# Feed forward of a hybrid diffusion step: tensor operations moved from GpSimd to VectorE and ScalarE, second weights prepared in the first product, loads issued ahead of splits

## Chip, cores and metric

The kernel runs on one core of one Trainium2 chip. The metric is the time of the device in microseconds (us). PE is TensorE, DVE is VectorE, ACT is ScalarE, POOL is GpSimd, SP is SyncE, whose only work here is to issue loads.

## What is computed

One layer over 128 context tokens and 2048 latent tokens, in fp32. A norm, a projection, three groups of mixing (gated linear attention, a depthwise convolution, chunked gating) and an output projection come first; the change is nearly all in what follows:

```python
h = rmsnorm(x, norm2_g) * (1 + scale2) + shift2
x = x + gate2 * (jnp.square(jax.nn.relu(h @ w_ff1)) @ w_ff2)   # 1024 -> 4096 -> 1024
y = rmsnorm(x, final_g)
```

## The kernel before

**Arithmetic.** Each fp32 operand is split into two halves in the fast matmul format: ACT copies it rounded (`hi`, an ACT CAST in the profile), and a subtraction gives the rest (`lo`). A product takes three matmuls (`mm3`: hi by hi, hi by lo, lo by hi). Both products of the feed forward use a seven-product scheme for 2x2 blocks in place of eight products, so that sums and differences of blocks are operands too.

**First product** (`ff1_units`, tiles `T`/`u` and `v`). Two groups of tokens, g = 0 and 1, times 16 column blocks i of `w_ff1`. One such turn has seven products p0 to p6 of 4 units of 3 matmuls, 84 matmuls of 512 columns; in group 0 a turn has 24 more of 256 columns for the context tokens (`ff1_context`). All seven read right operands made of tokens, which stay for a whole group (`right_operand`, tiles T for p0 to p3, u for p4 to p6), and left operands made of weights, which are new for each turn (`left_operand`: two loads into `raw`, the sums, four splits into `v`). The results lie in four banks z: p0, p2, p4 and p6 write one and the same bank, p3 and p5 another one, p1 a bank g. After each product ACT or DVE takes the bank away (`after(p)`: copies by ACT after p0, p2 and p3, additions by DVE after p1, p4 and p5). p4 can't begin before the copy after p2 is done, nor p6 before the addition after p4. Squares of the positive part, then three combinations of blocks (`comb`, on GpSimd) follow, and stores of the tiles fx, fy, fz to `f_d`.

**Second weights** (`w2_prep`). `w_ff2` times gate2 and its block combinations are made on GpSimd, 16 times (2 operations of 128x1024, 4 of 128x512, 7 stores to `w_d`), 3 times in group 1 of the first product and 13 times in the second product.

**Second product** (`ff2_units`, tiles `o`, `s`). Eight parts c of the hidden columns times four groups b of tokens, 84 matmuls each, and 24 more per c for the context tokens (`context`). Every operand is loaded from `f_d` or `w_d` and split (`operand`, lines 1405 and 1406; the subtraction goes to DVE or GpSimd by a rule). After each product DVE adds the bank to the sum of its tokens (line 1510, two for each p). Two of the z banks are held by the context tokens.

**Order.** `weave(units, items)` runs items between the units of the matmuls at hand-written positions; a scheduler then orders each engine's instructions, which the engine runs in that order. SP issues loads in the order of the program, and a load waits in SP's queue for its buffer. Stores go through POOL's queue. The relations that matter most are these two, from `weave` and `after`:

```python
while items and items[0][0] <= i:
    items.pop(0)[1]()          # a position of an item is a number of units
u()
bank = (za, gb, za, zc, za, zc, za)   # which bank p0 to p6 write
```

Of the kernel before, what the change touches and what calls it, by code (L numbers as in the profile page):

```python
# [43 lines left out]
def tile_hybrid(  # L44
# [62 lines left out]
    def raw():  # L107
        return rawp.tile([P, D], F32, tag="raw", name="raw", bufs=3)
# [4 lines left out]
    def cacc():  # L113
        return rawp.tile([P, D], F32, tag="cacc", name="cacc", bufs=2)
# [646 lines left out]
    def stage(t):  # L761
# [415 lines left out]
    def split_in_place(hi, lo, eng=V):  # L1177
        S.copy(out=hi, in_=lo.bitcast(F32))
        eng.tensor_tensor(out=lo, in0=lo.bitcast(F32), in1=hi.bitcast(F32), op=ALU.subtract)

    def right_operand(g, i, kk, dst):

        unit = tunit if i < 4 else uunit
        hi, lo = unit(), unit()
        ld_in_order(out=lo.bitcast(F32).rearrange("p (k n) -> p k n", k=2), in_=tb_d[g][:, i, 2 * kk:2 * kk + 2])
        split_in_place(hi, lo, G if kk else V)
        dst[i, kk] = (hi, lo)

    for t in range(NT - 2, -1, -1):
# [4 lines left out]
        if t in (3, 1, 0):  # L1194

            items += [((10 if t else 5) + 4 * kk, lambda kk=kk, i={3: 0, 1: 1, 0: 2}[t]: right_operand(0, i, kk, TB[0]))
                      for kk in range(2)]
# [21 lines left out]
    def left_operand(i):  # L1219

        w, rw, sf = {}, {}, {}
# [6 lines left out]
        def plain(r):  # L1228
            hi, lo = wunit(), wunit()
            split(hi, lo, rw[r])  # L1230
            w[r] = [x.rearrange("p (k f n) -> p k f n", k=4, f=2) for x in (hi, lo)]

        def sums(r):
            a1, a2 = (rw[x].rearrange("p (k f n) -> p k f n", k=4, f=2) for x in range(2))
            sf[r] = cacc()
            s_ = sf[r].rearrange("p (k f n) -> p k f n", k=4, f=2)
            if r == 0:

                V.tensor_tensor(out=s_[:, :, 0], in0=a1[:, :, 1], in1=a2[:, :, 1], op=ALU.add)
                V.tensor_tensor(out=s_[:, :, 1], in0=s_[:, :, 0], in1=a1[:, :, 0], op=ALU.subtract)  # L1240
            else:

                s2_ = sf[0].rearrange("p (k f n) -> p k f n", k=4, f=2)[:, :, 1]
                V.tensor_tensor(out=s_[:, :, 0], in0=a1[:, :, 0], in1=a1[:, :, 1], op=ALU.subtract)
                V.tensor_tensor(out=s_[:, :, 1], in0=a2[:, :, 0], in1=s2_, op=ALU.subtract)

        def mixed(r):
            hi, lo = wunit(), wunit()
            split(hi, lo, sf[r])
            w[2 + r] = [x.rearrange("p (k f n) -> p k f n", k=4, f=2) for x in (hi, lo)]  # L1250

        return w, [lambda: load(0), lambda: load(1), lambda: plain(0), lambda: plain(1),
                   lambda: sums(0), lambda: mixed(0), lambda: sums(1), lambda: mixed(1)]


    LEFT = ((0, 0), (1, 0), (2, 1), (2, 0), (3, 0), (3, 1), (1, 1))

    def ff1_units(g, i, w, tb):
# [12 lines left out]
        def square(x):  # L1271
            stt(x, x, 0.0, x, ALU.max, ALU.mult)

        def comb(out, a, b, op):
            G.tensor_tensor(out=out, in0=a, in1=b, op=op)  # L1275

        def after(p):
            if p == 0:
                S.copy(out=f00, in_=za)
            elif p == 1:  # L1280
                V.tensor_tensor(out=f00, in0=f00, in1=gb, op=ALU.add)
# [5 lines left out]
            elif p == 4:  # L1287
                V.tensor_tensor(out=f11, in0=fy[:, 0], in1=za, op=ALU.add)  # L1288
                square(f11)
            elif p == 5:  # L1290
                V.tensor_tensor(out=f01, in0=f01, in1=zc, op=ALU.add)
                square(f01)
                V.tensor_tensor(out=fy[:, 0], in0=f01, in1=f11, op=ALU.add)
# [359 lines left out]
```

## Time and profile before

| what | value |
|---|---|
| median of 3 runs | 2496.91 us (2488.81 to 2501.26) |
| profiled execution, its own time | 2490.42 us |
| its span, first to last instruction | 2488.7 us |
| mean granted TensorE clock | 0.967 |
| busy PE, DVE, POOL, ACT | 91%, 72%, 42%, 39% of the span |
| moved by DMA | 437.99 MB, mean 176 GB/s |

The feed forward takes the span from some 976 us on: group 0 of the first product until some 1361 us, group 1 until 1727 us, then the second product. An engine's share is an average over these stages, and a matmul's busy time includes its pipeline, so what a stage could gain is read from PE's waits and from the pace of its matmuls.

### The profile page before, as it was taken

Reading aid. Unit: us, or ns where it says so; the run is one execution under the profiler, and the core shown is the slowest. Engines: PE = TensorE matmul, PEld = TensorE weight load, DVE = VectorE, ACT = ScalarE, POOL = GpSimd, SP = SyncE. Lnnn points to the kernel's source line nnn. Section 1 sums busy time; section 2 is a strip of 40 time slices with the busy share of each in tenths; the row PEclk is TensorE's granted clock in tenths of the full one; section 3 lists DMA queues with packets and bytes.
Section 4 is the critical chain, followed back from the end, with each engine's and each line's share of the span. In section 5 each row is a group of like instructions: output and inputs, shape, how many; then the busy total and the mean of one; then the engine's idle time right before and its main releaser. Section 6 shows DMA issues by size and latency. Waiting matters only on the chain. (4 is left out here: it accounts for less than half of the span.)

```text
span 2488.7 us, 32998 instructions
## 1 busy us (share of the span) xinstructions
PE 2271.3 (91%) x12018; PEld 1854.0 (74%) x12018; DVE 1801.8 (72%) x2702; ACT 974.9 (39%) x1787; POOL 1055.8 (42%) x982
## 2 busy tenths in 40 slices
PE   6999999999988998899999789888889989989996
PEld 5788887777766776688887568677678777778775
DVE  5987755878887865677776787775667766677677
ACT  4666764333344465333333323222233233233242
POOL 2332325444424454333334454433655545545632
PEclk9999999999989999899999999999999999999999
DMA  8656635333445467333446345447666456456554
GB/s 283 235 196 200 218 103 172 121 126 125 139 148 196 144 221 250 123 128 122 140 138 219 133 153 169 157 148 263 213 208 218 165 186 198 166 192 203 173 203 144
DMA packets 217731, 437.99 MB, mean 176 GB/s; under 512 B 17525, under 2 KB 118175, under 8 KB 213984
## 3 DMA queue, kind: packets, MB, share of 16 engines
q1 hardware_dynamic: 171456, 263.57, 31.9%
q0 software_dynamic: 46112, 172.31, 19.8%
q8 instruction: 95, 1.56, 0.3%
q14 instruction: 68, 0.56, 0.1%
HBM read 270.39 MB, written 165.43 MB: 175 GB/s over the span
## 5 line engine op out<-in xcount | busy, mean ns | idle before, releaser
L131 PE MATMUL z<-w,hb 128*128 128x512 f32 (+1 forms) x2486 | 556.8, 370 | 14.7 <-ACT hb L776 8.8
L131 PEld LDWEIGHTS z<-w,hb 128*128 128x128 f32 x2486 | 418.6, 191 | 90.3 <-ACT hb L776 9.0
L131 PE MATMUL z<-u,v 128*128 128x512 f32 x1152 | 288.6, 407 | 57.3 <-DVE fz L1288 28.2
L131 PEld LDWEIGHTS z<-u,v 128*128 128x128 f32 x1152 | 224.5, 197 | 114.6 <-DVE fz L1288 31.8
L1405 ACT CAST o<-o 128x1024 fp32r<-128x1024 f32 x148 | 155.4, 1051 | 366.4 <-DMA o<-f_d 248.4
L131 PE MATMUL z<-T,v 128*128 128x512 f32 x1152 | 280.4, 395 | 10.4 <-ACT v L176 5.5
L1275 POOL TENSOR_TENSOR fz<-fx,fy 128x512 f32<-128x512 f32 x64 | 117.6, 1837 | 364.5 <-DVE fy L67 336.8
L131 PE MATMUL g<-o 128*128 128x512 f32 x1116 | 270.6, 391 | 0.5 <-DVE o L1406 0.5
L1510 DVE TENSOR_TENSOR T<-T,z 128x512 f32<-128x512 f32 x256 | 171.6, 682 | 137.0 <-PE z L131 136.9
L131 PE MATMUL z<-o 128*128 128x512 f32 x1080 | 265.1, 394 | 2.6 <-DVE T L1510 1.5
L131 PEld LDWEIGHTS z<-T,v 128*128 128x128 f32 x1152 | 216.7, 190 | 56.0 <-ACT v L176 5.7
L131 PEld LDWEIGHTS g<-o 128*128 128x128 f32 x1116 | 211.1, 189 | 45.4 <-DVE o L1406 1.0
L131 PEld LDWEIGHTS z<-o 128*128 128x128 f32 x1080 | 205.7, 191 | 48.5 <-DVE T L1510 3.2
L67 DVE SCALAR_TENSOR_TENSOR cacc<-xp,wd,cacc 128x512 f32<-128x512 f32 (+2 forms) x360 | 241.3, 724 | 0.1
L131 PE MATMUL z<-o,s 128*128 128x512 f32 x576 | 157.2, 417 | 55.7 <-DVE T L1510 27.4
L131 PE MATMUL z<-w,T 128*128 128x512 f32 x720 | 182.1, 406 | 6.0 <-ACT T L776 3.7
L1406 DVE TENSOR_TENSOR o<-o 128x1024 fp32r<-128x1024 f32 x96 | 165.8, 1729 | 20.8 <-ACT o L1405 20.5
L131 PEld LDWEIGHTS z<-o,s 128*128 128x128 f32 x576 | 113.2, 200 | 89.3 <-DVE T L1510 29.9
L1510 DVE TENSOR_TENSOR T<-T,g 128x512 f32<-128x512 f32 x192 | 130.0, 683 | 63.0 <-PE g L131 62.3
L131 PEld LDWEIGHTS z<-w,T 128*128 128x128 f32 x720 | 136.1, 194 | 34.6 <-ACT T L776 3.9
L1406 POOL TENSOR_TENSOR o<-o 128x1024 fp32r<-128x1024 f32 x52 | 128.2, 2475 | 60.9 <-ACT o L1405 60.5
L177 DVE TENSOR_TENSOR v<-cacc,v 128x1024 fp32r<-128x1024 f32 x64 | 78.2, 1222 | 103.4 <-ACT v L176 103.4
(312 smaller groups left out, 3608.6 us busy)
## 6 DMA issues: line engine op xcount, KB each, us to landing
o<-f_d SPq DMA_DIRECT2D x93, 512.0 KB
raw<-in_w_ff_dram SPq DMA_DIRECT2D x68, 512.0 KB
w_d<-T POOLq DMA_DIRECT2D x112, 256.0 KB, 3.1
o<-w_d SPq DMA_DIRECT2D x55, 512.0 KB
f_d<-fz POOLq DMA_DIRECT2D x32, 768.0 KB, 5.9
raw<-in_w_mod_dram SPq DMA_DIRECT2D x32, 512.0 KB
f_d<-fy POOLq DMA_DIRECT2D x32, 512.0 KB, 4.0
f_d<-fx POOLq DMA_DIRECT2D x32, 512.0 KB, 3.6
```

What stands on the lines that cost most here:

```text
L67: return V.scalar_tensor_tensor(out=out, in0=in0, scalar=scalar, in1=in1, op0=op0, op1=op1)
L131: tc.keep_in_program_order(T.matmul(out, lhsT, rhs, start=start, stop=stop, skip_group_check=read))
L177: order(V.tensor_tensor(out=lo, in0=src, in1=hi.bitcast(F32), op=ALU.subtract))
L1275: G.tensor_tensor(out=out, in0=a, in1=b, op=op)
L1405: S.copy(out=hi, in_=src)
L1406: eng.tensor_tensor(out=lo, in0=src, in1=hi.bitcast(F32), op=ALU.subtract)
L1510: V.tensor_tensor(out=y, in0=y, in1=bank, op=ALU.add)
```

## The change

GpSimd keeps the stores and small powers for the norms; its large tensor operations in the output projection and the feed forward go to DVE, and some squares from DVE to ACT. The sums of left operands are made in place, in `raw`. All 16 preparations of second weights go into the first product (12 in group 0, turns 3 to 14; 4 in group 1, turns 2, 5, 8, 11), in tiles `cacc`. Loads and splits become two separate steps, the load some 4 to 8 units ahead. The context products of the second product come four to a part c, two each in b = 1 and b = 2, and the first operands of the second product are made in the last turn of the first, in tiles T, raw and cacc.

```diff
-            G.tensor_tensor(out=ml, in0=mt, in1=mh.bitcast(F32), op=ALU.subtract)
+            V.tensor_tensor(out=ml, in0=mt, in1=mh.bitcast(F32), op=ALU.subtract)
...
-        split_in_place(hi, lo, G if kk else V)
+        return load, lambda: split_two(*box)
...
+        def sums():
+            (a11, a21), (a12, a22) = ([four(rw[r])[:, :, f] for f in range(2)] for r in range(2))
+            V.tensor_tensor(out=a22, in0=a21, in1=a22, op=ALU.add)
+            V.tensor_tensor(out=a21, in0=a11, in1=a21, op=ALU.subtract)
+            V.tensor_tensor(out=a11, in0=a22, in1=a11, op=ALU.subtract)
+            V.tensor_tensor(out=a12, in0=a12, in1=a11, op=ALU.subtract)
...
-    LEFT = ((0, 0), (1, 0), (2, 1), (2, 0), (3, 0), (3, 1), (1, 1))
+    LEFT = ((0, 0), (1, 0), (2, 0), (3, 1), (2, 1), (3, 0), (1, 1))
...
         def square(x):
-            stt(x, x, 0.0, x, ALU.max, ALU.mult)
+            act(x, x, AF.Relu)
+            act(x, x, AF.Square)
         def comb(out, a, b, op):
-            G.tensor_tensor(out=out, in0=a, in1=b, op=op)
+            V.tensor_tensor(out=out, in0=a, in1=b, op=op)
...
-                V.tensor_tensor(out=f10, in0=f10, in1=f10, op=ALU.mult)
+                act(f10, f10, AF.Square)
...
-                box.append(unit())
+                box.append(cacc())
...
-            for x in box:
-                G.tensor_tensor(out=x, in0=x, in1=g2, op=ALU.mult)
+            V.tensor_tensor(out=box[f], in0=box[f], in1=g2f, op=ALU.mult)
...
-            G.tensor_tensor(out=y, in0=w, in1=y, op=ALU.subtract)
...
+                V.tensor_tensor(out=o, in0=a, in1=b, op=op)
                 st.dma_start(out=d_[:, p], in_=o)
...
-        x = operand(w2_d[c][:, :, p], unit, V if c == 0 or p in (1, 3, 5, 6) else G)
...
-        x = operand(s, unit if n < 3 else sunit, G if n == 1 and c + b else V)
...
-            if g == 1 and i in (4, 8):
-                items += zip((3, 10, 22), w2_prep(i // 4 - 1, lambda: tunit(F32), g2f)[1:])
+            if g == 0 and 3 <= i < 15:
+                items += zip((1, 5, 9, 16, 30), w2_prep(i - 3))
+            elif g == 1 and i in (2, 5, 8, 11):
+                items += zip((1, 4, 8, 12, 17), w2_prep(12 + i // 3))
...
-                items += [(4 * p + 4.5 + kk, lambda p=p, kk=kk: right_operand(1, p, kk, TB[1])) for p, kk in ORDER]
+                ops = [(12.5 + 4 * p + kk, right_operand(1, p, kk, TB[1])) for p in range(7) for kk in range(2)]
+                late_ops = [(x + d, f) for x, o in ops for d, f in zip((0, 4.5), o)]
+                items += [o for o in late_ops if o[0] < 36]
+                after_first = [(x - 36, f) for x, f in late_ops if x >= 36]
```

**DVE in a turn of group 0.** Before, one turn from the split of a summed left operand on (`cacc` holds the sums, line 1288 is the addition after p4):

```order
L177 TENSOR_TENSOR v<-cacc,v 128x1024
L1239 TENSOR_TENSOR cacc<-raw 128x4x128
L1288 TENSOR_TENSOR fz<-fy,z 128x512
L1240 TENSOR_TENSOR cacc<-cacc,raw 128x4x128
L67 SCALAR_TENSOR_TENSOR fz<-fz 128x512
L1291 TENSOR_TENSOR fy<-fy,z 128x512
L67 SCALAR_TENSOR_TENSOR fy<-fy 128x512
L177 TENSOR_TENSOR v<-cacc,v 128x1024
```

Now, in a turn with a preparation of second weights (lines 1387 and 1395; `cacc` holds those weights; the third row is the split of the second loaded left operand, the last row the addition after p4):

```order
L1283 TENSOR_TENSOR fz<-fx,fy 128x512
L1387 TENSOR_TENSOR cacc<-cacc,raw 128x1024 x2
L1179 TENSOR_TENSOR v<-raw,v 128x1024
L1283 TENSOR_TENSOR fx<-fx,g 128x512
L1249 TENSOR_TENSOR raw<-raw 128x4x128
L1395 TENSOR_TENSOR cacc<-cacc 128x512
L1250 TENSOR_TENSOR raw<-raw 128x4x128
L1395 TENSOR_TENSOR cacc<-cacc 128x512
L1251 TENSOR_TENSOR raw<-raw 128x4x128
L1395 TENSOR_TENSOR cacc<-cacc 128x512
L1283 TENSOR_TENSOR fz<-fy,z 128x512
```

Six operations of the preparation now stand on DVE ahead of the addition after p4.

**ACT at the start of the first product.** Before (u are the right operands of p4 to p6, lines 1284 and 1286 the copies after p2 and p3):

```order
L1178 CAST u<-u 128x1024
L1284 COPY fy<-z 128x512
L1178 CAST u<-u 128x1024
L1286 COPY fy<-z 128x512
L64 ACTIVATE raw<-g,modc,s_4873 128x128 x2
L1178 CAST u<-u 128x1024
```

Now (lines 1292 and 1294 are these copies):

```order
L1287 COPY fx<-z 128x512
L1178 CAST v<-raw 128x1024 x2
L64 ACTIVATE fx<-fx 128x512 x2
L1178 CAST u<-u 128x1024 x6
L1178 CAST v<-raw 128x1024
L1292 COPY fy<-z 128x512
L1294 COPY fy<-z 128x512
```

All six casts of u, and one of the next turn, now stand ahead of the copy after p2.

**POOL before and DVE now in the second product.** Before, POOL (lines 1377 to 1387 prepare second weights, 1406 splits operands):

```order
L1406 TENSOR_TENSOR o<-T,o 128x1024
L1377 TENSOR_TENSOR T<-T,cacc 128x1024
L1378 DMA w_d_205<-T 128x512
L1406 TENSOR_TENSOR o<-o 128x1024 x4
L1377 TENSOR_TENSOR T<-T,cacc 128x1024
```

Now, DVE (line 1539 adds banks z and g to the sums, 1179 splits operands):

```order
L1539 TENSOR_TENSOR T<-T,g 128x512 x2
L1179 TENSOR_TENSOR o<-raw,o 128x1024
L1539 TENSOR_TENSOR T<-T,z 128x512 x2
L1179 TENSOR_TENSOR o<-o 128x1024
L1539 TENSOR_TENSOR T<-T,g 128x512 x2
L1539 TENSOR_TENSOR T<-T,z 128x512 x2
L1179 TENSOR_TENSOR o<-o 128x1024
L1179 TENSOR_TENSOR s<-s 128x512
L1539 TENSOR_TENSOR T<-T,z 128x512 x2
```

Nothing of this is left on POOL, and DVE has a split after nearly every pair of additions.

## Rows read from the trace of the kernel before

**Rows 1.** The page, part 1: busy time, share of the span, instructions.

```profile
PE 2271.3 (91%) x12018; PEld 1854.0 (74%) x12018; DVE 1801.8 (72%) x2702; ACT 974.9 (39%) x1787; POOL 1055.8 (42%) x982
```

**Rows 2.** Stretches: us; busy PE, PEld, DVE, ACT, POOL (x instructions); PE clock; DMA share, GB/s.

```profile
700.00:976.00 276.00, 241.99 (x1118) 194.25 (x1117) 209.41 (x348) 141.66 (x282) 118.52 (x117) 0.94 0.54 184
976.00:1014.00 38.00, 25.60 (x88) 18.24 (x88) 24.39 (x25) 17.93 (x26) 16.55 (x10) 0.77 0.49 174
1014.00:1344.00 330.00, 330.00 (x1640) 280.72 (x1640) 231.91 (x249) 102.93 (x149) 119.39 (x104) 0.99 0.41 136
1344.00:1400.00 56.00, 35.90 (x128) 25.62 (x127) 41.21 (x34) 21.33 (x26) 29.02 (x17) 0.89 0.56 206
1400.00:1729.00 329.00, 299.25 (x1270) 244.13 (x1269) 247.02 (x241) 96.26 (x123) 138.81 (x115) 0.95 0.50 169
1729.00:1756.00 27.00, 14.77 (x47) 10.36 (x46) 16.43 (x19) 13.89 (x16) 6.34 (x6) 0.76 1.04 385
1756.00:2393.00 637.00, 591.41 (x2522) 480.98 (x2520) 440.60 (x524) 184.85 (x196) 351.21 (x245) 0.98 0.57 192
2393.00:2489.00 96.00, 75.13 (x305) 58.79 (x305) 72.74 (x131) 34.16 (x77) 20.91 (x21) 0.94 0.42 144
```

**Rows 3.** Timeline, PE, two products in a row: start, us, engine, operation, count.

```profile
1548.58 2.88 PE L131 MATMUL z<-T,v 128*128 128x512 f32 x12
...
1551.30 2.88 PE L131 MATMUL g<-T,v 128*128 128x512 f32 x12
```

**Rows 4.** Groups by line: busy us, mean ns of one | idle before them, releaser.

```profile
L1275 POOL TENSOR_TENSOR fz<-fx,fy 128x512 f32<-128x512 f32 x64 | 117.6, 1837 | 364.5 <-DVE fy L67 336.8 <-DVE fx L1299 27.5
L1510 DVE TENSOR_TENSOR T<-T,z 128x512 f32<-128x512 f32 x256 | 171.6, 682 | 137.0 <-PE z L131 136.9
...
L177 DVE TENSOR_TENSOR v<-cacc,v 128x1024 fp32r<-128x1024 f32 x64 | 78.2, 1222 | 103.4 <-ACT v L176 103.4
...
L176 ACT CAST v<-raw 128x1024 fp32r<-128x1024 f32 x64 | 67.0, 1053 | 105.4 <-PE z L131 85.8 <-issue 16.2 <-DMA raw<-in_w_ff_dram 3.4
...
L1293 DVE TENSOR_TENSOR fy<-fy,fz 128x512 f32<-128x512 f32 x32 | 54.8, 1713 | 0.0
...
L1240 DVE TENSOR_TENSOR cacc<-cacc,raw 128x512 f32<-128x512 f32 x32 | 21.9, 685 | 0.0
```

**Rows 5.** Timeline around a stop of PE in group 1 of the first product.

```profile
1470.71 6.89 SPq L137 DMA_DIRECT2D raw<-in_w_ff_dram  x2
...
1474.24 2.95 DVE L177 TENSOR_TENSOR v<-raw,v 128x1024 fp32r<-128x1024 f32 x1
...
1483.68 0.69 DVE L1239 TENSOR_TENSOR cacc<-raw 128x512 f32<-128x512 f32 x1 [4.04 <-DMA raw<-in_w_ff_dram]
...
1485.03 5.49 PE L131 MATMUL z<-u,v 128*128 128x512 f32 x12 [9.85 <-DVE fz L1288]
```

**Rows 6.** Timeline in the second product: a load and its cast, then a stop of PE.

```profile
2177.90 1.62 SPq L137 DMA_DIRECT2D T<-in_w_ff_dram  x2
...
2182.03 1.05 ACT L1405 CAST o<-T 128x1024 fp32r<-128x1024 f32 x1 [2.99 <-DMA T<-in_w_ff_dram]
...
2188.93 7.06 POOL L1406 TENSOR_TENSOR o<-o 128x1024 fp32r<-128x1024 f32 x3
...
2191.94 5.15 DVE L1406 TENSOR_TENSOR o<-o 128x1024 fp32r<-128x1024 f32 x1 [1.63 <-ACT o L1405]
...
2197.74 4.33 PE L131 MATMUL z<-o,s 128*128 128x512 f32 x12 [4.08 <-DVE T L1510]
```

**Rows 7.** PE's waits from 976 to 1400 us: total, times, longest.

```profile
PE z L131 <- POOL u L1179: 15.0, 4, 5.7
...
PE z L131 <- ACT v L176: 5.5, 1, 5.5
```

**Rows 8.** Timeline, PE's first wait in the second product.

```profile
1734.93 0.79 PE L131 MATMUL g<-o,T 128*128 128x512 f32 x1 [5.11 <-ACT o L1405]
```

**Rows 9.** DMA issues: KB each, median us from issue to landing.

```profile
w_d<-T POOLq DMA_DIRECT2D x112, 256.0 KB, 3.1
```

More of the change, by code (lines that the diff above doesn't have):

```diff
@@ L1402, in sunit, with operand @@
         return gp[0].tile([P, 512], dt, tag="s", name="s", bufs=6)
-    def split_two(hi, lo, src, eng):
-        S.copy(out=hi, in_=src)
-        eng.tensor_tensor(out=lo, in0=src, in1=hi.bitcast(F32), op=ALU.subtract)
-    def operand(src, unit, eng):
+    def operand(src, unit):
         hi, lo = unit(), unit()
@@ new lines, in w2_operand, with load @@
+        return two_steps(load)
+    def f_operand(c, b, n, out, unit=ounit):
+        def load():
+            g, ts = b // 2, slice(b % 2 * 256, b % 2 * 256 + 256)
+            ps = slice(2 * n, min(2 * n + 2, 7))
+            s = f_d[c][g][:, ps, :, ts].rearrange("p a q n -> p (a q) n")
+            x, f = operand(s, unit if n < 3 else sunit)
+            for a in range(s.shape[1]):
+                out[3 - a // 2 if n == 1 else 2 * n + a // 2, a % 2] = [y[:, a * 256:a * 256 + 256] for y in x]
+            return f
+        return two_steps(load)
@@ new lines, in fc_operand, with load @@
+    def fc_operand(c, out):
+        def load():
+            x, f_ = operand(fc_d[c].rearrange("p q f n -> p (q f) n"), sunit)
+            for q in range(2):
+                for f in range(2):
+                    out[f, q] = [y[:, (2 * q + f) * P:(2 * q + f + 1) * P] for y in x]
+            return f_
+        return two_steps(load)
+    units_ = {1: [raw, raw], 2: [raw, cacc]}
+    early = [((4.5, 9), f_operand(0, 0, 0, F, tunit)), ((8.5, 13), f_operand(0, 0, 1, F, tunit)),
+             ((12.5, 17), w2_operand(0, 0, w2, tunit)), ((16.5, 21), f_operand(0, 0, 2, F, tunit))]
@@ L1436, in tile_hybrid @@
+    early += [((x, x + 4), w2_operand(0, p, w2, lambda p=p: units_[p].pop(0)(F32R))) for x, p in ((1, 1), (3, 2))]
+    after_first = []
     for g in range(2):
@@ L1538, in tile_hybrid, with context, load, parts @@
     yc = [zbank(), zbank()]
[L1539 to L1542 removed]
+    def context(k, Fc):
         box = []
[L1546 to L1551 removed]
+        def load():
+            box.append(raw() if k >= 4 else tunit(F32))
+            ld_in_order(out=box[0], in_=w_ff2[0, k * P:(k + 1) * P, :])
+        def parts():
             box.extend([ounit(), ounit()])
[L1553 removed]
+            split_two(*box[1:], box[0])
         def unit(h):
             hs = (left, right)[h]
[L1557 to L1558 removed]
+            mm3(yc[h], *Fc[k % 2, k // 2 % 2], box[1][:, hs], box[2][:, hs], k == 0, k == 4 * NC_ - 1, True)
+            if k == 4 * NC_ - 1:
                 tmp = yl[0, 1]
@@ L1564, in unit @@
                     norms.append(0)
-        return weights, [lambda: unit(0), lambda: unit(1)]
-    w2_operand(0, 1, w2)
-    for p in range(2, 7):
-        w2_operand(0, p, w2)
-    f_operand(0, 0, 3, F)
-    fc_operand(1, Fc)
+        return load, parts, [lambda: unit(0), lambda: unit(1)]
+    first = [w2_operand(0, p, w2) for p in (3, 4, 6, 5)]
+    first[2:2] = [f_operand(0, 0, 3, F)]
+    first.append(fc_operand(0, Fc))
+    for f, _ in first:
+        f()
+    for _, f in first[:2]:
+        f()
+    begun = [f for _, f in first[2:]]
     raw4 = []
     for c in range(NC_):
-        w2n, F0 = {}, {}
+        w2n, F0, Fcn = {}, {}, {}
         more = c + 1 < NC_
@@ new lines, in tile_hybrid @@
+            if b < 3 or more:
+                cb, out = ((c, b + 1), Fn) if b < 3 else ((c + 1, 0), F0)
+                for at, n in zip(((1, 7), (8.5, 14), (16.5, 22), (18, 25)) if b < 3 else
+                                 ((0.5, 7), (8.8, 15), (16.8, 23), (22, 29)), range(4)):
+                    add(at, f_operand(*cb, n, out))
+            if b == 3 and more:
+                for at, p in zip(((4.5, 10), (8.5, 13), (12.5, 18), (16.5, 25.5), (20.5, 28), (24.5, 30)), (0, 1, 2, 3, 4, 6)):
+                    add(at, w2_operand(c + 1, p, w2n))
+                add((26, 31), fc_operand(c + 1, Fcn))
+                begun[:] = [begun[k] for k in (1, 0, 2, 3)]
```

226 lines of the change are left out of this document (100 added, 126 removed).

## The prediction

> **What bounds the kernel now.** I read the page first: PE is busy 91% of the span, DVE 72%, POOL 42% [rows 1]. That says that PE is the resource, but not what could be gained, since a matmul's busy time holds its pipeline. So I took PE's pace from a stretch without a wait: twelve matmuls of 512 columns start 2.72 us apart [rows 3], 0.2267 us each. Then I cut the span into stages and set each stage's length against its number of matmuls [rows 2]. The reader is to see in these rows that PE's lost time lies in the seams of the feed forward and in the parts where GpSimd prepares second weights, not in group 0 of the first product:
> - start of the first product, 976 to 1014: 38.0 - 88 x 0.2267 = 18.1 us lost;
> - group 0, 1014 to 1344: PE busy for all 330 us, nothing lost; its 15 turns take 330 / 15 = 22.0 us each;
> - switch of groups, 1344 to 1400: 56.0 - 128 x 0.2267 = 27.0;
> - group 1, 1400 to 1729: 329.0 - 1270 x 0.2267 = 41.1;
> - start of the second product, 1729 to 1756: 27.0 - 47 x 0.2267 = 16.3;
> - second product, 1756 to 2393: 637.0 - 2522 x 0.2267 = 65.3.
>
> Together 167.8 us. Part of it is waiting, part a lower granted clock: it stands at 0.76 to 0.98 in the stages with stops and at 0.99 in group 0, where PE never stops [rows 2], so a stop that goes gives back some clock too.
>
> What PE waits for is mostly DVE, and what makes DVE late is GpSimd. A DVE operation of 128x512 takes 685 ns alone, but the one that always runs beside GpSimd's combination (1293) takes 1713 ns [rows 4]. In the second product a split that takes 1222 ns alone took 5.15 us beside three splits of POOL in a row (7.06 us); the additions behind it came late, and PE stood for 4.08 us [rows 6]. In group 1 a split of 2.95 us held its raw tile, so the next load was issued late (the pair of issues ends at 1477.60), DVE stood at its first user until 1483.68, and PE, which needed the addition behind that, stood for 9.85 us [rows 5].
>
> **The change part by part.** The sum is made against the profiled execution, 2490.42 us, which is 6.5 us under the median of the runs.
>
> *Output projection, 700 to 976.* Seventeen subtractions go to DVE, 1.22 us each [rows 4], some 21 us on an engine that is busy 209 of 276 us [rows 2]. GpSimd's work there slowed DVE by a like amount, if rows 4 hold: 1.03 us for each POOL operation that DVE meets. I take 0, with 10 us to either side.
>
> *Start of the first product.* PE's waits for POOL's splits of u (part of 15.0 us, which the switch of groups shares) go; the wait for the first cast of v, 5.5 us, stays [rows 7], since what stands before that cast on ACT is the same. New is that ACT now makes six casts of u and one of v before it copies the bank of p2: 7 x 1.05 = 7.4 us [rows 4], of which one product (2.72 us, p3) covers PE. That is a new stop of 4.7 us. Of the 18.1 us I leave 10: a gain of **8**, between 0 and 12.
>
> *Group 0.* Nothing is to be gained here, so this can only cost. Each of 12 turns takes a whole preparation on DVE: 2 x 1.22 + 4 x 0.685 = 5.2 us. Without it DVE needs 12.6 us a turn (13 operations of 0.685, 3 splits of 1.22), with it 17.8 (18.3 where all four splits are whole), of 22.0: it fits. What could set the pace is a circle over the two cacc tiles: cast of a loaded weight 1.05; on DVE split 1.22, two combinations 1.37, two gates 2.44, split 1.22, addition 0.69, eight sums 5.48; landing of the last store 3.1 [rows 9]; then the load of cacc, 4.1 from issue to cast [rows 6], and behind it in SP's order the next raw, 512 KB more, 1.36 us at the 385 GB/s that a full stretch moved [rows 2]. That is 22.0 us, just the length of a turn, with no time for issuing. I take 0.5 us over, 6 us, and 2 us for bank copies that stand behind a cast on ACT: a loss of **8**, between 0 and 35.
>
> *Switch of groups.* The 14 splits of right operands were half POOL's and blocked ACT from their issue; now their loads stand ahead. A load can't begin before its product of the old group is done, and the copies after p2 and p3 still stand behind casts of T on ACT. With 4.1 us for a load and two casts the copy after p2 comes some 2 us late, twice; with the clock I leave 10 of 27.0: a gain of **17**, between 5 and 22.
>
> *Group 1.* Three preparations on POOL cost 41.1 / 3 = 13.7 us each at most (one stop is 9.85 us [rows 5]; after it the same matmuls run slower for a while). Four on DVE now: 17.8 us of the 84 x 0.2267 = 19.0 of a turn. The addition after p4 stands behind six operations of the preparation and behind the split of the second raw load. That load is issued when the last split frees its tile, at the end of a turn, and takes 6.1 us with three stores in flight [rows 5] to 4.1 alone [rows 6]; the operations from there to the addition sum to 12 us, so it comes 1 to 3 us after the 16.3 us at which p6 wants the bank. 4 x 3 with the clock, 3 for the rest: I leave 15 of 41.1, a gain of **26**, between 10 and 36.
>
> *Start of the second product.* The 5.11 us wait for the first operand [rows 8] goes, since p0 to p2 have theirs in T, raw and cacc, 8.2 us of cover. The next operands reuse space that the last turn leaves late, so I keep 5 of 16.3: a gain of **11**, between 4 and 14.
>
> *Second product.* POOL does nothing there but small powers. DVE per part c: 56 additions of 0.682, 23 whole and 5 half splits: 38.2 + 28.1 + 3.3 = 69.6 us, of (4 x 84 + 24) x 0.2267 = 81.6. A split stands between two pairs of additions, 1.22 + 1.37 = 2.6 us against the 2.72 of a product, so an addition is seldom late by over 1 us. No stores of weights and no 1 MB loads for them compete with loads of operands any more. I leave 3.3 us a part, 23 of 65.3 over seven: a gain of **42**, between 15 and 55. The last part keeps its tail of norms: 0.
>
> Sum: 8 - 8 + 17 + 26 + 11 + 42 = 96 us. 2490.4 - 96 = 2394 for a profiled execution, and with the 6.5 us of the median 2401; I say **2400 us**.
>
> **Rivals.**
> *A, slower: the circle in group 0 sets the pace.* For it: the sum above is as long as a turn, and a load beside stores took 6.1 us, not 4.1. With both DMA legs 2 us longer it is 26 us, 12 x 4 = 48 us, less the 8 taken: 2440 us. It decides the sign from 22.0 + (96 + 8) / 12 = 30.7 us on; at 32 us the kernel takes 2400 - 8 + 12 x 10 = 2512. Against it: 8.7 us more than the sum would need every DMA leg doubled, while the stage has a DMA share of 0.41 and would get some 0.8. The Trainium skill (DMA: Bandwidth & Descriptors, Queues, rings and completion order) says that each DMA engine takes turns between its queues packet by packet; by that a load with small packets gets the lesser part beside stores with large ones, and the circle would be nearer 26 us. Rows 5 and 6 agree in direction, 6.1 to 4.1 us.
>
> *B: DVE becomes the bound.* In b = 3 and b = 0 of a part DVE's list is about 19 us against 19.0 of PE, and it runs in order; each late cast then delays additions. At 2 x 3 us a part the second product gains nothing, and the preparations of group 1 cost 10 more: 2400 + 42 + 10 = 2452. For it: shares of 85 to 95%. Against it: durations without POOL beside them. The Trainium skill (Perfetto Trace Analysis, Optimizing Scalar/DVE Operations) speaks against the change in the same sense: with DVE saturated, some work may go to Scalar or even GpSimd, here the reverse is done; it adds that the two share a read port, so that such a move might not help. The trace bears out the second half (1713 for 685 ns) and not yet the first.
>
> *C: the stops were made by loads and their order, not by GpSimd.* In rows 5 the last thing waited for is a DMA. Then the stops of group 1 and of the switch stay, and 26 + 17 are not gained: 2443.
>
> *D: more goes than I say.* If half of the 71 us that I leave in these stages (10 + 8 + 10 + 15 + 5 + 23) goes too: 2365.
>
> **How the numbers follow.** Forecast 0.55, A at 26 us 0.07, A beyond 30.7 us 0.04, B 0.11, C 0.10, D 0.13. 2360 to 2450 takes in the forecast, A at 26 us, C, most of D and half of B, some 8 in 10. A measurement of this kernel can tell 0.5% from no change, 12.5 us. All cases but the far end of A are faster by more: 0.89; I give 0.05 to no change, for several losses together, and 0.06 to slower.
>
> **What would show it.** POOL's busy share falls to about half, and DVE's means stand near 0.69 and 1.22 us for all groups. DVE's share rises to 73 to 80%. Turns of group 0 lengthen from 22.0 to about 22.5 us; if 24 or more, the circle was underrated. PE still stands some 5 us in p4 of the first turn, behind the copy after p2. In group 1 four stops of 1 to 3 us, none of 10. A part c of the second product takes 83 to 86 us, where it took 91 (637 / 7). The forecast is wrong if DVE's operations stay long without POOL beside them, if PE's waits in the second product are for DVE as long as before, or if the loads' waits in group 1 stay near 10 us.

## The result, and the profile after

The changed kernel takes 2338.47 us (median of 4 runs, 2335.05 to 2339.66), the kernel before, run beside it, 2499.09: ratio 0.9358, 95% interval 0.9323 to 0.9393. That is 160 us faster, where 96 were forecast, and below the forecast range of 2360 to 2450. The profiled execution took 2335.05 us, its span is 2333.3.

Page, part 1, of the changed kernel, against [rows 1]:

```profile
PE 2226.3 (95%) x12018; PEld 1833.1 (79%) x12018; DVE 1759.0 (75%) x2880; ACT 1073.8 (46%) x1963; POOL 474.9 (20%) x692
```

POOL's share fell from 42% to 20%, to about half as forecast, and DVE's rose to 75%. DVE has 178 instructions more and is busy 43 us less. Part of that is not GpSimd's doing: four kinds of squares went from DVE to ACT, 100 us in the kernel before (lines 67, 1299 and 1334). The stretches of the changed kernel, between the matmuls that stand nearest to the borders of [rows 2] (columns as there):

```profile
700.00:953.40 253.40, 234.80 (x1121) 190.85 (x1119) 194.55 (x370) 141.63 (x282) 67.89 (x98) 0.97 0.59 202
953.40:983.00 29.60, 23.40 (x89) 17.95 (x90) 23.64 (x26) 20.68 (x30) 1.86 (x3) 0.83 0.56 195
983.00:1311.20 328.20, 327.74 (x1640) 278.36 (x1639) 244.52 (x312) 156.55 (x238) 87.15 (x144) 1.00 0.68 250
1311.20:1346.10 34.90, 31.55 (x127) 25.46 (x127) 30.71 (x36) 25.45 (x35) 2.74 (x4) 0.90 0.72 257
1346.10:1634.30 288.20, 286.13 (x1260) 235.99 (x1259) 200.90 (x266) 137.34 (x197) 48.48 (x73) 1.00 0.59 212
1634.30:1648.80 14.50, 12.81 (x56) 10.24 (x55) 9.25 (x12) 5.13 (x7) 2.22 (x3) 1.00 1.04 397
1648.80:2236.90 588.10, 577.77 (x2522) 473.51 (x2521) 465.02 (x596) 191.78 (x206) 0.00 (x0) 0.99 0.51 173
2236.90:2333.30 96.40, 74.96 (x306) 58.59 (x304) 73.50 (x135) 33.12 (x76) 10.32 (x17) 0.94 0.41 141
```

Every kernel here issues 12018 matmuls, at each number one of the same shape; only in the second product do some products stand in another order (the context's above all). So a stage is best compared between the starts of the matmuls of the same two numbers in each trace. That gives this table, in us (the last column ends 10 to 12 us before the end of the span):

| kernel | output projection | start of first product | group 0 | switch | group 1 | start of second product | second product, seven parts | last part |
|---|---|---|---|---|---|---|---|---|
| before | 276.1 | 39.2 | 329.5 | 55.8 | 326.9 | 29.4 | 637.5 | 84.2 |
| changed | 253.2 | 29.8 | 328.1 | 34.9 | 288.2 | 14.5 | 588.3 | 86.0 |
| difference | -22.9 | -9.4 | -1.4 | -20.9 | -38.7 | -14.9 | -49.2 | +1.8 |
| forecast | 0 | -8 | +8 | -17 | -26 | -11 | -42 | 0 |

The differences sum to 155.6 us, the spans differ by 155.4. Four terms are outside their bounds: the output projection, group 0, group 1 and, by 1 us, the start of the second product. One trace was taken of each kernel. Stages that an edit does not touch differ from trace to trace by up to 4.0 us in the last part, 3.3 in the switch, 2.8 in the second product, 2.4 in the output projection and 1.5 elsewhere; smaller differences below show nothing.

Groups by line of the changed kernel from 953 to 2333 us, on DVE:

```profile
L1539 DVE TENSOR_TENSOR T<-T,z 128x512 f32<-128x512 f32 x256 | 172.9, 683 | 69.6 <-PE z L131 68.4
L1179 DVE TENSOR_TENSOR v<-raw,v 128x1024 fp32r<-128x1024 f32 x112 | 136.7, 1222 | 35.5 <-ACT v L1178 33.0
L1283 DVE TENSOR_TENSOR fz<-fx,fy 128x512 f32<-128x512 f32 x64 | 44.1, 688 | 3.9 <-ACT fx L64 0.9
L1395 DVE TENSOR_TENSOR cacc<-cacc 128x512 f32<-128x512 f32 x64 | 44.0, 687 | 19.2 <-DMA w_d<-cacc 19.2
...
L1283 DVE TENSOR_TENSOR fy<-fy,fz 128x512 f32<-128x512 f32 x32 | 21.9, 685 | 0.1
```

Nearly all shapes stand at 0.69 and 1.22 us (the longest mean of this size, 749 ns, is in the norms). The last row is the addition that took 1713 ns in [rows 4] (line 1293 before), and the combinations, 1837 ns on POOL, take 688 here. PE's waits from 953 to 1346 us (start, group 0 and switch), then those of group 1:

```profile
PE z L131 <- ACT fy L1292: 5.8, 3, 3.3
PE z L131 <- ACT v L1178: 4.2, 1, 4.2
PE z L131 <- DVE v L1179: 4.2, 2, 2.6
```

```profile
PE z L131 <- DVE fz L1283: 2.1, 2, 1.6
```

The waits for POOL's u [rows 7] are gone, and group 1 has one real stop, not four. The stop in the first turn, behind six casts of u and one of v, lasts 2.0 us; the longest wait for such a copy, 3.3 us, is in the switch of groups (at 1315.44 us):

```profile
974.57 0.96 PE L131 MATMUL z<-u,v 128*128 128x512 f32 x3 [2.02 <-ACT fy L1292]
```

Here is the stop of group 1 in the timeline, in a turn that holds a preparation:

```profile
1549.17 0.69 DVE L1395 TENSOR_TENSOR cacc<-cacc 128x512 f32<-128x512 f32 x1 [1.78 <-DMA w_d<-cacc]
...
1552.04 0.69 DVE L1395 TENSOR_TENSOR cacc<-cacc 128x512 f32<-128x512 f32 x1 [1.57 <-DMA w_d<-cacc]
1552.64 0.69 DVE L1252 TENSOR_TENSOR raw<-raw 128x512 f32<-128x512 f32 x1
...
1553.25 0.68 DVE L1395 TENSOR_TENSOR cacc<-cacc 128x512 f32<-128x512 f32 x1
1553.85 0.68 DVE L1283 TENSOR_TENSOR fz<-fy,z 128x512 f32<-128x512 f32 x1
...
1554.59 2.11 PE L131 MATMUL z<-u,v 128*128 128x512 f32 x8 [1.64 <-DVE fz L1283]
```

The addition after p4 stands behind operations of the preparation, as the forecast had it, and these stand twice for the landing of a store of the tile that they overwrite. The rows show a second thing: DVE operations of 0.69 us start 0.60 us apart (1552.04, 1552.64; 1553.25, 1553.85). These durations overlap, so a sum of them is too long for such a row. It holds where neighbours do not need each other: where an operation reads the result of the one before it, as lines 1251 and 1252 in a turn without a preparation (1411.14, 1411.87), they start 0.73 us apart.

### The profile page after: what moved, and what is told of

Its sections match the earlier page's. It is cut to its first block, busy times and chain, and to the rows that moved or that the text cites. A ratio compares the mean times of both kernels' runs of the same rounds, so it can differ in the third digit from the quotient of the medians.

```text
span 2333.3 us, 32930 instructions
## 1 busy us (share of the span) xinstructions
PE 2226.3 (95%) x12018; PEld 1833.1 (79%) x12018; DVE 1759.0 (75%) x2880; ACT 1073.8 (46%) x1963; POOL 474.9 (20%) x692
## 3 DMA queue, kind: packets, MB, share of 16 engines
q1 hardware_dynamic: 175344, 277.73, 35.7%
## 4 chain that ended last, share of the span: by engine, by line
PE 58%; DVE 11%; issue 8%; DMA 4%; POOL 3%; ACT 3%; SPq 0%; POOLq 0%; DVEq 0%; ACTq 0%
PE z L131 42%; PE g L131 15%; DVE cacc L67 5%; DMA o<-f_d 2%; PE g L134 1%; DVE T L1539 1%; DVE T L67 1%; DVE uv L67 1%; DMA o<-w_d 1%; POOL s L166 1%; POOL mv L166 1%; DVE o L1179 1%; ACT osq L1093 0%; POOL ssq L166 0%; DMA f_d<-fz 0%
## 5 line engine op out<-in xcount | busy, mean ns | idle before, releaser
L131 PE MATMUL z<-u,v 128*128 128x512 f32 x1152 | 270.9, 393 | 7.9 <-ACT fy L1292 5.8
L131 PE MATMUL g<-o 128*128 128x512 f32 x1080 | 261.6, 391 | 0.0
L131 PE MATMUL z<-o 128*128 128x512 f32 x1044 | 254.8, 390 | 1.6 <-DVE T L1539 1.6
L131 PEld LDWEIGHTS z<-o 128*128 128x128 f32 x1044 | 196.3, 188 | 43.5 <-DVE T L1539 2.4
L67 DVE SCALAR_TENSOR_TENSOR cacc<-xp,wd,cacc 128x512 f32<-128x512 f32 (+2 forms) x360 | 218.7, 662 | 0.0
L1178 ACT CAST v<-raw 128x1024 fp32r<-128x1024 f32 (+1 forms) x128 | 127.5, 998 | 151.7 <-PE z L131 77.9
L1179 DVE TENSOR_TENSOR o<-o 128x1024 fp32r<-128x1024 f32 x146 | 178.1, 1221 | 19.5 <-ACT o L1178 18.8
L166 POOL TENSOR_TENSOR ssq<-ssq,mhalf 128x1 f32<-128x1 f32 x51 | 34.6, 679 | 703.7 <-DVE ssq L165 687.7
L1179 DVE TENSOR_TENSOR v<-raw,v 128x1024 fp32r<-128x1024 f32 (+1 forms) x128 | 147.7, 1155 | 40.0 <-ACT v L1178 37.2
L131 PE MATMUL z<-o,s 128*128 128x512 f32 x576 | 148.8, 401 | 21.7 <-DVE T L1539 12.8
L1539 DVE TENSOR_TENSOR T<-T,g 128x512 f32<-128x512 f32 x192 | 129.5, 683 | 37.0 <-PE g L131 35.6
```

The costliest lines, as they stand in the source:

```text
L67: return V.scalar_tensor_tensor(out=out, in0=in0, scalar=scalar, in1=in1, op0=op0, op1=op1)
L131: tc.keep_in_program_order(T.matmul(out, lhsT, rhs, start=start, stop=stop, skip_group_check=read))
L166: G.tensor_tensor(out=out, in0=out, in1=mhalf[:, 0:out.shape[-1]], op=ALU.pow)
L1178: S.copy(out=hi, in_=src)
L1179: V.tensor_tensor(out=lo, in0=src, in1=hi.bitcast(F32), op=ALU.subtract)
L1539: V.tensor_tensor(out=y, in0=y, in1=bank, op=ALU.add)
```

## The experiments

Two theories were to be told apart. **Engine**: GpSimd's operations were long and stretched VectorE's beside them; taking them off GpSimd gives most. **Order**: loads ahead of splits and the preparations' new place give most (rival C). Stage lengths of all runs stand in a table at the end of this section. A time without an interval is that of one execution.

### Engine alone, order alone

The kernel before with VectorE in place of GpSimd in lines 777, 1186, 1275, 1377 to 1387, 1417, 1426 and 1588, nothing moved:

```diff
-            G.tensor_tensor(out=ml, in0=mt, in1=mh.bitcast(F32), op=ALU.subtract)
+            V.tensor_tensor(out=ml, in0=mt, in1=mh.bitcast(F32), op=ALU.subtract)
-        split_in_place(hi, lo, G if kk else V)
+        split_in_place(hi, lo)
...
```

> The kernel before with one thing changed: every tensor operation that the change takes from GpSimd (the conversion L777, the second casts of the right operands, the three combinations L1275, the preparations L1377 to L1387, the subtractions of the splits in the second product) is issued on VectorE. Order of loads, places of preparations and squares stay. Theory 1 (GpSimd's operations were slow and slowed VectorE's beside them; taking them off it gives most): 2400 us, 2380 to 2425, that is 80 to 120 of the 160 us gained, 15 to 22 us of it in the output projection and 15 to 30 us in group 1; VectorE's 128x512 addition L798 of the output projection falls from 1041 to about 690 ns. Rival (the new order gives most: loads ahead of splits, preparations in the first product): 2460 us or more, VectorE now late in the second product where preparations and splits share it.

Measured: 2424.01 us beside 2500.64 before, ratio 0.968 (0.9655 to 0.9705), 77 us. The reverse, the changed kernel with the same operations on GpSimd in its new order (`V` to `G` in the conversion, `right_operand` for kk = 1, the three last `comb` of a turn, `w2_prep`, and the splits that POOL had in the second product):

> The changed kernel with all the moved tensor operations (conversion, second casts of the right operands, the three combinations, preparations, the splits' subtractions of the second product) put back on GpSimd in the new order. The engine alone, in the old order, was worth 77 us. If engine and order simply add, 77 us are given back: 2415 us, 2400 to 2430. If the new order needs the faster engine (in group 0 a preparation of six operations at 1.8 to 3.6 us, some 15 us on GpSimd, in the circle over the two cacc tiles), more: 2450 to 2520, with group 0 longer by 40 to 110 us. If order alone gives most: 2375 or less.

Measured: 2436.83 us beside 2506.38, ratio 0.9733 (0.9707 to 0.9759), 70 us, between the case that the two add and the case that the order needs the engine. So neither theory takes it all: each half alone gives 70 to 77 us, and together 160. By stage they divide differently (table). The output projection is the engine's alone: 255.2 with the engine, 275.9 with the order. Group 1 has most of its gain from either: 297.3 and 304.4, from 326.9 (the two together 288.2). The start of the first product comes with either, and over half of the switch with each. The second product is hardly the engine's: 629.2 with the engine alone, and 593.1 with the order and GpSimd's splits. In group 0 the order without the engine costs 43.8 us.

### Output projection

One line, in either kernel: the subtraction of the conversion, on VectorE or GpSimd.

> The kernel before with the conversion L777 alone moved to VectorE. Theory 1: output projection 12 to 22 us shorter, total 2475 to 2487 us. Rival: under 5 us, total 2492 or more. My forecast's reading (VectorE takes on what GpSimd gives up, sum within 10 us either way) would show as 0 to 10.

> The changed kernel with the conversion L777 alone put back on GpSimd. Theory 1: the output projection (from 700 us to the same matmul as the 976 us point of before) gets 12 to 22 us longer than in the changed kernel and L798's mean is back at about 1.0 us; total 2350 to 2362 us. Rival (the loads ahead of the right operands' splits, or their second casts moved from GpSimd, gave this term): under 5 us, total 2338 to 2345.

Measured: in the kernel before 2479.84 us, stage 256.8 in place of 276.1; in the changed kernel 2362.77 us, 275.1 in place of 253.2. All other stages stay within 2.8 us. This one line is nearly the whole term of the output projection (19.3 of 22.9 us one way, 21.9 the other), as the engine theory says. VectorE is busy 210.0 us of this stage in the kernel before and 193.1 with the line moved, though that brings it 20.7: GpSimd's 17 operations, 43.1 us, had cost it 37.7, or 2.2 each. But is GpSimd's result late, or is VectorE slowed? The next run leaves the conversion on VectorE and gives GpSimd an operation whose result nobody waits for soon (it doubles the residual, so what this kernel computes is no longer the layer):

```diff
-            V.tensor_tensor(out=ml, in0=mt, in1=mh.bitcast(F32), op=ALU.subtract)
+            V.tensor_tensor(out=ml, in0=mt, in1=mh.bitcast(F32), op=ALU.subtract); x = staged[t][2]; G.tensor_tensor(out=x, in0=x, in1=x, op=ALU.add)
```

> The changed kernel (conversion on VectorE) with one more tensor operation on GpSimd at the place of every conversion: the residual tile x, loaded a turn ahead and not wanted for some 10 us, is added to itself (128x1024, so the residual that the output projection adds is doubled). Nothing waits for its result soon, and every engine's order is otherwise that of the changed kernel. If GpSimd's operation takes VectorE's time by running beside it: output projection 15 to 22 us longer than the changed kernel's 253 us, VectorE's addition L798 back at a mean near 1.0 us. If the conversions on GpSimd were only late results: 0 to 5 us longer, L798 near 690 ns.

Measured: stage 277.8, 24.6 longer than the changed kernel's; total 2365.39 us. The same groups of DVE, first of the changed kernel from 700 to 953 us, then of this run from 704 to 980 us, with POOL's operation of this run below (it carries the line of the conversion):

```profile
L67 DVE SCALAR_TENSOR_TENSOR cacc<-xp,wd,cacc 128x512 f32<-128x512 f32 (+1 forms) x149 | 78.6, 584 | 0.0
L798 DVE TENSOR_TENSOR w<-T,w 128x512 f32<-128x512 f32 x30 | 20.6, 687 | 0.4
...
L777 DVE TENSOR_TENSOR T<-T 128x1024 fp32r<-128x1024 f32 x15 | 18.2, 1215 | 2.6 <-ACT T L776 2.6
```

```profile
L67 DVE SCALAR_TENSOR_TENSOR cacc<-xp,wd,cacc 128x512 f32<-128x512 f32 (+1 forms) x145 | 95.2, 712 | 0.0
L777 DVE TENSOR_TENSOR T<-T 128x1024 fp32r<-128x1024 f32 x15 | 27.2, 1814 | 2.5 <-ACT T L776 2.5
L798 DVE TENSOR_TENSOR w<-T,w 128x512 f32<-128x512 f32 x30 | 22.7, 756 | 1.2 <-DVE T L797 0.4
```

```profile
L777 POOL TENSOR_TENSOR w<-w 128x1024 f32<-128x1024 f32 x17 | 33.3, 1970 | 7.3 <-DMA w<-in_x_sample_dram 7.2
```

Lateness of a result is out: an operation that nobody waits for costs as much. VectorE loses 145 x 0.128 + 15 x 0.599 + 30 x 0.069 = 29.6 us in these groups, beside 33.3 us of GpSimd. I had expected line 798 to be hit, as with the conversion on GpSimd (a mean of 1039 ns); here it is the conversion and, as there, the convolution (line 67): what stands beside GpSimd's operation is hit. How it reaches PE, in the timeline: the convolution takes 4.77 us beside two of GpSimd's operations, the conversion behind it is late, and PE stands for it.

```profile
795.99 4.77 DVE L67 SCALAR_TENSOR_TENSOR cacc<-xp,wd,cacc 128x512 f32<-128x512 f32 x1
796.44 3.75 POOL L777 TENSOR_TENSOR w<-w 128x1024 f32<-128x1024 f32 x2
...
800.68 1.21 DVE L777 TENSOR_TENSOR T<-T 128x1024 fp32r<-128x1024 f32 x1
...
801.94 9.62 PE L131 MATMUL z<-w,T 128*128 128x512 f32 x34 [2.05 <-DVE T L777]
```

PE's waits for the conversion, in the changed kernel (700 to 953 us) and here (704 to 980 us):

```profile
PE z L131 <- DVE T L777: 0.5, 1, 0.5
```

```profile
PE z L131 <- DVE T L777: 10.9, 4, 4.4
```

Another way to lose the time, GpSimd's small powers coming later behind the new operation, does not show: ACT's waits for them at line 806 are 15.8 us here and 16.4 in the changed kernel.

### The circle in group 0

> The changed kernel with the preparations of the second weights alone on GpSimd (two products of 128x1024 and four sums of 128x512 per preparation), in the new place. My forecast's circle (22.0 us with 5.2 us of VectorE in it) would become 22.0 - 5.2 + 14.6 = 31.4 us: group 0 longer by 9.3 us in each of 12 turns, 110 us, total near 2450. If the circle has room (it was overestimated by some us), group 0 longer by 0 to 60 us. Group 1 has four preparations only: 0 to 8 us longer.

> The changed kernel with four more VectorE operations of 128x1024 (maximum of a tile with itself, twice per cacc tile) in each preparation, 4.5 us of VectorE in the circle over the two cacc tiles. By my forecast's circle of 22.0 us against a turn of 22.1 the turns of group 0 become 26.5 us: 12 x 4.4 = 53 us longer. If the circle is really 2 to 3 us shorter: 18 to 30 us longer. If it has 5 us of room or more: 0 to 8 us.

The edits: `G` for `V` in both operations of `w2_prep`; and this:

```diff
         def gate(f):
+            for _ in range(2):
+                V.tensor_tensor(out=box[f], in0=box[f], in1=box[f], op=ALU.max)
             V.tensor_tensor(out=box[f], in0=box[f], in1=g2f, op=ALU.mult)
```

Measured: preparations on GpSimd, 2396.12 us, group 0 52.0 longer, 4.3 in each of 12 turns; four more operations on VectorE, 2378.4 us, group 0 18.0 longer, 1.5 a turn in the mean (turns from 22.2 to 28.1 us, where all turns with a preparation but one take 22.2 in the changed kernel).

The first of these runs does not test the circle: the engines wait next to nothing there for loads of cacc (0.3 us). What makes its turns longer is VectorE beside GpSimd. Groups by line from 985 to 1365 us, on POOL and on DVE:

```profile
L1395 POOL TENSOR_TENSOR cacc<-cacc 128x512 f32<-128x512 f32 x48 | 62.1, 1305 | 0.6
L1387 POOL TENSOR_TENSOR cacc<-cacc,raw 128x1024 f32<-128x1024 f32 x24 | 57.2, 2405 | 0.2
```

```profile
L1179 DVE TENSOR_TENSOR v<-raw,v 128x1024 fp32r<-128x1024 f32 (+1 forms) x60 | 121.1, 2019 | 46.9 <-ACT v L1178 45.8
L1251 DVE TENSOR_TENSOR raw<-raw 128x512 f32<-128x512 f32 x15 | 37.2, 2482 | 0.5
```

Splits and sums take up to 3.6 times their length. The addition after p1 stands behind them, ACT waits 98.2 us for it (39.0 in the changed kernel), and the copy after p2, which ACT makes, stands behind that; PE's waits in group 0 are all for this copy:

```profile
PE z L131 <- ACT fy L1292: 33.8, 12, 3.4
```

In the second run VectorE does stand for the loads of cacc (17.6 us in the changed kernel), and PE waits 10.3 us for additions after p4:

```profile
DVE cacc L1388 <- DMA cacc<-in_w_ff_dram: 24.1, 13, 4.8
```

Here 4.5 us more cost 1.5, so a turn of 22.2 us had some 3.0 us of room. If the circle is what used it up, it is about 19 us long, not 22.5. That is an estimate: VectorE was busy some 17.3 us of such a turn and is now busy 20.6 of 23.7 at the mean, so with its waits its own list is nearly full too, and the runs do not tell the two apart. Group 1 has no such room: the same four operations in four turns made it 20.0 longer, 5 us each.

### Group 1: one operation kind at a time

> The changed kernel with the three combinations per turn alone back on GpSimd. If they are what made the stops of group 1 (1.84 us each instead of 0.68, and VectorE slowed beside them, one buffer for fz): group 1 from 288 to 300 us or more, total 2350 to 2365. If it was the rest (order of the left operand, squares, second casts): 0 to 5 us. Group 0 within 3 us either way.

> The changed kernel with three of the four squares per turn on VectorE again (0.68 us each) instead of one more operation on ScalarE. If VectorE has no room at the ends of the turns: group 1 5 to 15 us longer, group 0 longer by up to 10 us through the circle over the cacc tiles. If it has room: within 3 us.

Measured: combinations on GpSimd, 2341.41 us, group 1 3.7 longer; three squares on VectorE again, 2337.87 us, group 1 4.6 longer and the start and the switch together 5.1 shorter. Both small: put back alone in the new order, neither kind brings the stops of group 1 back. All of them together on GpSimd cost 16.2 us there (304.4). In the old order the engine alone was worth 29.6 us there, as PE's waits show, first those in group 1 of the kernel before (1400 to 1729 us) and of that with everything on VectorE (1363 to 1661 us):

```profile
PE z L131 <- DVE fz L1288: 23.6, 7, 9.9
PE z L131 <- ACT fy L1286: 6.1, 1, 6.1
```

```profile
PE z L131 <- DVE fz L1288: 7.2, 4, 3.4
PE z L131 <- ACT fy L1284: 0.2, 1, 0.2
```

In the kernel before, the two stops of 9.9 us make up 19.7 of these 23.6 us: the one of [rows 5], and this one. Each ends 29 us after a preparation on GpSimd began (at 1455.8 and 1545.6 us).

```profile
1574.94 5.07 PE L131 MATMUL z<-u,v 128*128 128x512 f32 x12 [9.88 <-DVE fz L1288]
```

With everything on VectorE four short waits are left, 7.2 us. Only two of them, of 1.5 us, stand in the turn of a preparation, so they are not the four stops that I had forecast. The new order leaves 2.1.

### The second product

Each load again in front of its own split (below), and then, in another run, the whole old schedule of the second product, with its splits on VectorE and the preparations left in the first product:

```diff
-                items.append((x, steps[0]))
                 if y < 28:
+                    items.append((y, steps[0]))
                     items.append((y, steps[1]))
                 else:
-                    begun.append(steps[1])
+                    begun.append(lambda: both(steps))
...
```

> The changed kernel with each load of the second product's parts issued directly in front of its own split again, at the split's place, nothing else changed. If the loads ahead of the splits are what the second product gained (6 us per part beyond what the engine gave), parts go from 82.5 back to 86 to 90 us: 25 to 50 us longer, total 2365 to 2390. Rival (the preparations that left the second product gave it): 0 to 10 us, total under 2350.

> The changed kernel with the second product scheduled as in the kernel before (every load directly in front of its split, one part of the context per part, the old positions of the second weights' operands), but all splits on VectorE and without the preparations, which stay in the first product. If the preparations that left the second product (their loads, six operations and seven stores per two parts) gave its gain: parts of 82 to 85 us, total 2338 to 2365. If the order of loads, splits and context gave it: parts of 87 to 90 us as in the kernel before with everything on VectorE, total 2375 to 2400.

Measured: without the lead 2356.91 us, the seven parts only 3.6 longer, but the last part 15.0 longer (PE waits 13.0 us for casts there, none in the changed kernel), so the lead in this sense is worth little where a part follows. The old schedule took 2365.41 us, just over what the first reading allowed; its parts of 86.8 us are just under what the second did. So both count, and the runs give one path through it, from which another order of the steps could take somewhat different shares: seven parts 637.5 before, 629.2 with everything on VectorE, 607.8 with the preparations gone as well, 588.3 with the new schedule; the start 29.4, 34.0, 24.8, 14.5. Engine 8, preparations 21, schedule 20 us. PE's waits from 1660.8 to 2324 us in the second of these kernels and from 1634 to 2266.6 in the third, then in the changed kernel (1634.3 to 2237.1 us):

```profile
PE z L131 <- DVE o L1406: 27.6, 8, 6.0
PE z L131 <- DVE T L1510: 16.6, 9, 2.8
...
```

```profile
PE z L131 <- DVE o L1179: 25.9, 9, 4.3
PE z L131 <- ACT o L1178: 7.6, 1, 7.6
PE g L131 <- DVE o L1179: 4.4, 2, 2.7
```

```profile
PE z L131 <- DVE T L1539: 8.4, 7, 4.3
PE g L131 <- DVE o L1179: 1.7, 1, 1.7
PE z L131 <- DVE o L1179: 1.7, 1, 1.7
```

With the preparations gone the waits for additions (16.6 us) go. With the schedule the waits for splits fall from 30.3 to 3.4 us, and 8.4 us of waits for additions are there again. Whether it is the preparations' loads and stores or their operations that cost 21 us was not tried apart.

### An edit on top

> The changed kernel with two edits of its own order: the splits of the right operands 4 to 6 of the first turn come one by one inside that turn instead of all ahead of it, and the last part of the second product alternates its two row tiles over the first four products. If ScalarE's copy behind six casts makes the stop in the first turn: start 2 to 4 us shorter (29.8 to 26 to 28). If a bank that is added too late makes the stops of the last part: that part (86 us with the tail of 10) 4 to 8 us shorter. Else both within 1 us.

Splits of i = 4 to 6 became items at 7 to 17 of the first turn; the last part alternates its row tiles over p0 to p3. Measured: 2335.68 us, within the changed kernel's own runs. The start is 3.6 us shorter, as the stop behind six casts said, and PE has no wait for that copy there. The last part is 1.8 longer, where 4 to 8 us less were expected: that its stops come from a bank added too late is not borne out. No run beats the changed kernel by more than can be measured.

| kernel | output projection | start | group 0 | switch | group 1 | start of second | seven parts | last part |
|---|---|---|---|---|---|---|---|---|
| before, conversion on VectorE | 256.8 | 39.2 | 329.3 | 57.3 | 327.7 | 29.8 | 640.3 | 85.3 |
| before, everything on VectorE | 255.2 | 31.2 | 328.7 | 44.7 | 297.3 | 34.0 | 629.2 | 89.5 |
| changed, everything on GpSimd | 275.9 | 29.4 | 371.9 | 41.9 | 304.4 | 14.5 | 593.1 | 85.3 |
| changed, conversion on GpSimd | 275.1 | 30.4 | 328.2 | 34.2 | 288.9 | 14.5 | 588.5 | 87.3 |
| changed, extra GpSimd operation | 277.8 | 29.2 | 328.4 | 35.7 | 288.9 | 14.5 | 588.5 | 89.1 |
| changed, preparations on GpSimd | 255.6 | 30.2 | 380.1 | 36.1 | 289.2 | 14.5 | 588.4 | 90.0 |
| changed, four operations more | 254.6 | 30.1 | 346.1 | 34.6 | 308.2 | 14.4 | 588.4 | 89.8 |
| changed, combinations on GpSimd | 255.4 | 30.2 | 327.3 | 34.6 | 291.9 | 14.5 | 587.2 | 88.8 |
| changed, squares on VectorE | 255.5 | 26.9 | 327.3 | 32.7 | 292.8 | 14.5 | 588.1 | 88.0 |
| changed, no lead of loads | 254.6 | 30.0 | 327.3 | 37.2 | 288.2 | 14.5 | 591.9 | 101.0 |
| changed, old second product | 254.5 | 30.1 | 327.3 | 35.6 | 287.7 | 24.8 | 607.8 | 86.8 |
| changed, splits spread | 255.6 | 26.2 | 327.4 | 33.9 | 287.7 | 14.4 | 588.3 | 87.8 |

## Why the prediction was wrong, and where it was right

The sign and much of the mechanism were right; the time was 62 us too long. Step by step:

- **Output projection, 0 within 10: the step that failed most, 22.9 gained.** It priced GpSimd's work at 1.03 us of VectorE for each operation, 17.5 us, against the 21 us that come to VectorE, and took that for a wash. The runs show about twice that price: 2.2 us for each conversion, 1.7 (29.6 / 17) for each extra operation. The 1.03 is what one operation of VectorE loses in [rows 4]; here the convolution alone loses 20.5 us and line 798 another 10.6 beside the 17 conversions. And the sum asked only for VectorE's busy time, while PE waits for single late operations. In [rows 2] the stage has a clock of 0.94 and PE busy 242 of 276 us, and I never asked what PE waited for there: its waits sum to 34.0 us, and to 18.6 after. The runs with one line moved show nearly the whole term, and the extra operation shows why.
- **Group 0, 8 lost: 1.4 gained.** Turns with a preparation take 22.2 us, as those without one do. The sum of 22.0 us and 0.5 was too long, by some 3 us if the circle is what the run with four operations more filled. It added durations that overlap (15 VectorE operations, some 0.09 us each where they do not need each other, by the timeline above); the rest of the difference was not taken apart. By the Trainium skill's rule on packets (DMA: Bandwidth & Descriptors, Queues, rings and completion order), as I had used it, the circle would have been 26 us. Then each microsecond that is added would have shown, and in that run a third of them did (1.5 of 4.5). The store of the weights took 3.4 us at the median after, 3.1 before [rows 9].
- **Group 1, 26 within 36: 38.7 gained.** Mechanism right, size off: of the four stops that I left, one of over 1 us came, and the clock went from 0.95 to 1.00, where I had left 15 us of loss and 2.4 stayed. Why three of the four additions came in time was not taken apart. The price for a preparation on GpSimd was counted wrong too: the kernel before makes two of them in group 1, not three (the third begins at 1753.7 us, in the second product, which has 14), so a stop of 9.9 us belongs to each.
- **Switch 17 (20.9), start of the first product 8 (9.4), last part 0 (+1.8): right.** The stop in the first turn for the copy after p2 is there, but with 2.0 us where 4.7 was worked out; spreading the casts takes 3.6 us off the stage. In the switch the copy after p2 is late once, by 3.3 us, where it was to be some 2 us late twice. Start of the second product: 11 forecast, 14.9 measured, just past its bound of 14.
- **Second product, 42: 49.2. The number was near for a reason that was half wrong.** I read [rows 6] as GpSimd's splits holding up VectorE, and that is what they do; but with everything on VectorE in the old order only 8 of the 49 us went, and with GpSimd's splits in the new order only 4.8 came back, although DVE's splits there took 1413 ns at the mean. The preparations that left and the new schedule gave the rest, so that the number came near is in good part luck. Rival C's reason, the order, holds for much of this stage. Its forecast, that the stops of group 1 and of the switch stay, fell, and for the output projection it has nothing.
- **Rivals.** A fell (group 0 did not lengthen); that a circle over the cacc tiles can set the pace is suggested by the run with four operations more, not shown apart from a full VectorE. B fell: DVE's share rose to 75%, and PE's waits for it shrank. The Trainium skill says that moving work of a saturated VectorE to GpSimd may make sense, with the caveat that the two share a read port, so that it might not help (Perfetto Trace Analysis, Optimizing Scalar/DVE Operations). The runs agree with the caveat: 33.3 us of GpSimd cost VectorE 29.6. D, that half of the 71 us left goes too, was nearest: 2365 for 2338. Of those 71 us some 29 went; the rest of the miss is the output projection and group 0, which D leaves as forecast.

## What to carry to other kernels

Before work goes to GpSimd, ask what VectorE does at that moment: in this kernel's output projection an operation there was paid almost once more in VectorE's time (37.7 us for 43.1, and 29.6 for 33.3), whether or not anybody waited for it, and it costs the kernel only where VectorE's next result is awaited (the combinations on GpSimd alone cost group 1 only 3.7 us). Look for PE's waits in every stage that a moved operation runs in, not only in the stages that the change is about. When a forecast comes out near, undo its halves all the same: here the second product was forecast to 7 us, and its reason was GpSimd for one sixth.

## What was not expected of the hardware

- VectorE beside GpSimd is hit far harder than the 1713 for 685 ns of [rows 4] when two of GpSimd's operations stand in a row. In group 0 of the changed kernel with everything on GpSimd (groups by line, 1004 to 1376 us) the first sum of a left operand takes six times its length, and in the timeline one of them ends just after two operations of GpSimd do:

```profile
L1249 DVE TENSOR_TENSOR raw<-raw 128x512 f32<-128x512 f32 x15 | 60.2, 4014 | 0.5
```

```profile
1216.71 6.19 DVE L1249 TENSOR_TENSOR raw<-raw 128x512 f32<-128x512 f32 x1
...
1217.61 4.73 POOL L1387 TENSOR_TENSOR cacc<-cacc,raw 128x1024 f32<-128x1024 f32 x2
```

- GpSimd's own operations differ as much: 1970 ns for the extra one of 128x1024 in the output projection, 2405 for the preparations' of the same size. What makes the difference was not tried.
- VectorE's operations of 128x512 last 0.69 us each in the profile. In a row they start 0.60 us apart if they do not need each other, and some 0.73 if one reads the result of the other.
